# Neighbourhood attention with token tiles of sixteen rows by eight columns

## The chip, the core and the metric

The kernel runs on one core of a Trainium2 chip, with its five engines: TensorE (PE in the profile; PEld is its weight load), VectorE (DVE), ScalarE (ACT), GpSimd (POOL) and SyncE (SP), which mostly issues transfers. What is measured is the device time of one execution in microseconds. Lower is better.

## What is computed

Two layers of an encoder over 1024 tokens of width 1024. The tokens are a grid of 16 rows by 64 columns, counted row by row. Each layer takes one input projection apart into three mixers (latent attention MLA, six heads; neighbourhood attention NA, six heads; differential attention, four heads) and a gate for each, and ends with one output projection and a residual. What the change touches is NA:

```python
def neighborhood_attention(q, k, v, rpb, scale):
    kr = min(NA_KR_MAX, rows)          # 8 of 16 rows
    kc = NA_KC                         # 16 of 64 columns
    col_start = jnp.clip(col - kc // 2, 0, GRID_W - kc)
    col_idx = col_start[:, None] + jnp.arange(kc)[None, :]
    dc = col_idx - col[:, None] + (NA_KC - 1)
    def one(r):
        r0 = jnp.clip(r - kr // 2, 0, rows - kr)
        k_r = lax.dynamic_slice_in_dim(kg, r0, kr, axis=1)[:, :, col_idx]
        v_r = lax.dynamic_slice_in_dim(vg, r0, kr, axis=1)[:, :, col_idx]
        dr = r0 + jnp.arange(kr) - r + (NA_KR_MAX - 1)
        bias = rpb[:, dr[:, None, None], dc[None, :, :]]
        s = jnp.einsum('bchd,brcjhd->bhcrj', q_r, k_r) * scale
        s = s + bias.transpose(0, 2, 1, 3)[None]
        p = jax.nn.softmax(s.reshape(B, H, GRID_W, kr * kc), axis=-1)
        return jnp.einsum('bhcrj,brcjhd->bchd', p, v_r)
```

So a query at row r and column c sees 8 rows by 16 columns of keys, with a bias by relative row and column. MLA and the differential attention see all 1024 keys with rotary embeddings by token number.

## The kernel before

**Tiles and stages.** A tile is 128 consecutive tokens, two grid rows, and there are eight. A layer runs through: input norm and latent projection; differential and key-value projections; differential attention with the gate's projection beside it; NA projections; NA; MLA; output projection. In the first layer the start is apart: eight tiles of x are loaded (L376), squared and scaled (L352, L354), transposed by PE (`start_turn`, L355 to L360) and modulated (`start_mod`), while the modulation's weights stream in on SP's queue. The rope table is one transfer of 128x8x32 on SP (L405).

**NA.** `NA_CHUNKS` (L39) gives each of the eight query tiles its first key tile and their count, 4 or 5, 36 a head in all. An item (`na_item`, L1000) is one head and one query tile. `first`: scores into PSUM S in two halves, two matmuls each (L1012 with the high part of the keys, L1013 with the low part); VectorE adds the table and finds the extreme (L1018); ScalarE takes the exponential with its sum (L1021); VectorE the reciprocal (L1023); GpSimd scales (L1024). `second`: PE transposes the probabilities, 128 columns at a time (L638), into PSUM T, and ScalarE copies them out (L138), a second time where there are five. `third`: the value matmuls (L1042), one per key tile, whose result is 64 rows, so that they use 64 of PE's 128 columns: those of the head's parity. `finish`: after four items VectorE multiplies the gate by the result (L1048). PSUM O holds one head's half at a time.

`na_table` (L951) makes a head's bias and mask table: two transfers (L963) on SP from `rpb_rep` in memory, GpSimd adds the column mask (L964), copies ten of the fourteen rows (L965) and fills what the inner tiles must not see (L966 to L968). Even heads use the buffers t4 and t2, odd heads the two raw buffers; so a table's buffer comes free when head h-2 has its last scores. `rpb_rep` is written earlier, in the differential projections, by one transfer a head on ScalarE's queue (L480), which repeats the bias 64 times. `na_forms` (L971) transposes queries and keys of the next head through PSUM F (L982, L996), and ScalarE and VectorE write their high and low parts (L983, L984, L138, L998).

**What sets the order.** The items are registered with keys by `at`, first 3 places ahead of second, a table 6 places ahead of its head, forms 4 ahead; a scheduler then places each engine's instructions by its own estimate of times. MLA's setup (`mla_setup`, L1071: two subtractions on GpSimd at L1094, the query table's transfer and scaling at L1098 and L1099) and its first head's forms stand among the last NA heads.

## Time and profile before

| | us |
|---|---|
| median of 3 runs (lowest, highest) | 1851.77 (1850.18, 1853.68) |
| profiled execution, its own time | 1856.72 |
| its span in the trace | 1854.9 |

| engine | busy us | share of the span |
|---|---|---|
| PE | 1720.4 | 93% |
| DVE | 1338.3 | 72% |
| ACT | 947.9 | 51% |
| POOL | 811.2 | 44% |

Times in the rows are microseconds from the span's start. Busy time of an engine is the union of its instructions; a PE timeline's "us" is the whole passage of a group, and since matmuls overlap, what a group costs PE is read from one start to the next.

### The profile page before, as it was taken

How to read it: one execution, taken by the hardware profiler on the slowest of the kernel's cores; microseconds unless marked ns; L12 is line 12 of the kernel's file. 1: busy time of each engine (PE TensorE's matmuls, PEld its weight loads, DVE VectorE, ACT ScalarE, POOL GpSimd, SP SyncE). 2: the span in 40 equal slices, each digit the busy share in tenths (PEclk: the TensorE clock that was granted, in tenths of full speed). 3: DMA queues.
4: the chain of work that ended last, by engine and by line, in shares of the span. 5: the costliest groups of instructions: out<-in, count | busy, mean ns of one | idle time of the engine just before them, and what ended most of it. 6: DMA issues, size and time to landing. Idle time of an engine off the chain costs nothing. (4 is left out here: it accounts for less than half of the span.)

```text
span 1854.9 us, 28846 instructions
## 1 busy us (share of the span) xinstructions
PE 1720.4 (93%) x10724; PEld 1471.2 (79%) x10724; DVE 1338.3 (72%) x2634; ACT 947.9 (51%) x1954; POOL 811.2 (44%) x756
## 2 busy tenths in 40 slices
PE   4998889989899999989998988899999999999998
PEld 3978667778798888978878877777889888898877
DVE  6879877765975679995576487778565656999742
ACT  6522577771057667753342227777512765776500
POOL 4422435533345545473225043555415564556532
PEclk9999899999999999999999989999999999999999
DMA  9356000104323101131232520001221140003022
GB/s 285 100 131 168 13 24 23 35 1 123 104 55 54 59 1 24 35 89 33 80 127 59 109 82 23 24 12 35 66 86 29 21 102 1 12 24 81 23 91 91
DMA packets 141036, 117.60 MB, mean 63 GB/s; under 512 B 39834, under 2 KB 126048, under 8 KB 140384
## 3 DMA queue, kind: packets, MB, share of 16 engines
q1 hardware_dynamic: 116716, 103.61, 19.1%
q0 software_dynamic: 12480, 6.29, 2.0%
q10 hardware_dynamic: 11700, 5.85, 1.7%
q8 instruction: 85, 1.39, 0.3%
q14 instruction: 55, 0.45, 0.1%
HBM read 97.91 MB, written 23.68 MB: 66 GB/s over the span
## 5 line engine op out<-in xcount | busy, mean ns | idle before, releaser
L138 ACT ACTIVATE R<-T 128x512 fp32r<-128x512 f32 (+1 forms) x336 | 180.8, 550 | 125.5 <-PE T L638 61.8
L620 PE MATMUL F<-R,Pb 128*128 128x512 f32 x766 | 233.8, 420 | 11.7 <-ACT sg L138 11.7
L620 PEld LDWEIGHTS F<-R,Pb 128*128 128x128 f32 x766 | 141.5, 197 | 48.3 <-ACT sg L138 18.6
L1182 POOL TENSOR_SCALAR Pb<-Pb,sm 128x1024 f32<-128x1024 f32 x96 | 110.4, 1151 | 138.3 <-DVE sm L1178 69.3
L731 DVE TENSOR_REDUCE sm<-S 128x1 f32<-128x1024 f32 x128 | 153.2, 1218 | 16.0 <-PE S L726 14.5
L653 DVE TENSOR_TENSOR R<-T,R 128x512 fp32r<-128x512 f32 x192 | 129.1, 681 | 21.0 <-ACT R L138 20.1
L1180 ACT ACTIVATE Pb<-S,sm,rs_q 128x1024 f32<-128x1024 f32 x96 | 115.6, 1204 | 30.1 <-DVE sm L1178 26.4
L1200 PE MATMUL O<-R,nd 128*128 128x256 f32 x768 | 118.3, 292 | 6.3 <-DVE R L653 6.2
L1042 PE MATMUL O<-R,n1v 128*64 128x128 f32 x864 | 120.0, 280 | 1.2 <-ACT R L138 1.2
L1177 DVE TENSOR_REDUCE sm<-S 128x1 f32<-128x1024 f32 x96 | 116.5, 1213 | 5.4 <-PE S L1174 5.2
L650 PE MATMUL T<-ident,Pb 128*128 128x128 f32 x768 | 112.1, 275 | 6.8 <-DVE R L653 6.8
L1024 POOL TENSOR_SCALAR Pb<-Pb,sm 128x512 f32<-128x512 f32 (+1 forms) x96 | 74.5, 780 | 93.2 <-DVE sm L1023 87.7
L1200 PEld LDWEIGHTS O<-R,nd 128*128 128x128 f32 x768 | 102.9, 191 | 13.3 <-DVE R L653 9.1
L1042 PEld LDWEIGHTS O<-R,n1v 128*64 128x64 f32 x864 | 91.1, 136 | 21.7 <-issue 11.1
L1306 POOL TENSOR_TENSOR raw<-sg,raw 128x512 fp32r<-128x512 f32 x32 | 50.0, 1562 | 120.4 <-DVE raw L1305 120.3
L650 PEld LDWEIGHTS T<-ident,Pb 128*128 128x128 f32 x768 | 89.8, 142 | 16.1 <-DVE R L653 5.0
L801 POOL TENSOR_TENSOR Pb<-raw,Pb 128x512 fp32r<-128x512 f32 x32 | 43.8, 1372 | 125.2 <-DVE Pb L800 87.9
L733 ACT ACTIVATE nd<-S,sm 128x1024 f32<-128x1024 f32 x64 | 71.4, 1116 | 47.9 <-DVE sm L731 47.0
L457 ACT ACTIVATE t<-T 128x512 f32<-128x512 f32 x32 | 19.2, 599 | 141.9 <-DVE n1k L933 73.3
L737 POOL TENSOR_SCALAR nd<-nd,sm 128x1024 f32<-128x1024 f32 x48 | 58.7, 1223 | 65.0 <-DVE sm L735 64.8
L733 ACT ACTIVATE sg<-S,sm 128x1024 f32<-128x1024 f32 x64 | 71.3, 1115 | 27.7 <-DVE sm L731 14.1
L1172 PE MATMUL S<-R 128*128 128x512 f32 x192 | 84.8, 443 | 0.3
(439 smaller groups left out, 5247.4 us busy)
## 6 DMA issues: line engine op xcount, KB each, us to landing
raw<-in_w_in_dram SPq DMA_DIRECT2D x32, 512.0 KB
t<-in_ada_w_dram SPq DMA_DIRECT2D x40, 256.0 KB
n1k<-in_w_out_dram SPq DMA_DIRECT2D x16, 512.0 KB
v_d<-n1k SPq DMA_DIRECT2D x16, 384.0 KB
nl<-in_ada_w_dram SPq DMA_DIRECT2D x24, 256.0 KB
nd<-v_d POOLq DMA_DIRECT2D x12, 512.0 KB, 4.9
rpb_rep<-in_na_rpb_dram ACTq DMA_DIRECT2D x12, 476.2 KB
R<-in_ada_w_dram SPq DMA_DIRECT2D x8, 512.0 KB
```

Source lines behind the costliest of these rows:

```text
L138: A.activation(o, i, AF.Copy, scale=scale)
L620: ins = fn()
L650: PE.transpose(pt[:, i * 128:(i + 1) * 128], src_cols(i), ident)
L653: V.tensor_tensor(lo4, pv, f(hi4), ALU.subtract)
L731: V.tensor_reduce(stt[:, m:m + 1], ps, AX.X, ALU.max, negate=True)
L733: A.activation(p, ps.rearrange("p (k n) -> p k n", k=8), AF.Exp, bias=stt[:, m:m + 1], accum_out=stt[:, 2 + m:3 + m])
L1042: PE.matmul(O[m:m + 64, qs], nv[:, c0 + i, h * 64:(h + 1) * 64], PTf[qb][:, i, qs], start=(i == 0), stop=(i == n - 1), skip_group_check=True)
L1172: PE.matmul(o, qhi[:, ts_], khi[:, ks], start=True, stop=False)
L1177: V.tensor_reduce(stt[:, 0:1], ps, AX.X, ALU.max, negate=True)
L1180: A.activation(p, ps, AF.Exp, bias=stt[:, 3:4], scale=rs, accum_out=stt[:, 1:2])
L1182: mla["g"] = G.tensor_scalar(p, p, stt[:, 2:3], 0.0, ALU.mult, ALU.add)
L1200: PE.matmul(box["o"], mla[f"v{e}"][:, k], mla["PT"][b][:, hl, k], start=(k == 0 and hl == 0), stop=(k == 7 and hl == 1))
```

## The change

The order of tokens inside the kernel changes: a tile is now eight grid columns by all sixteen rows (`token_tiles`), in which the token number is column group, row, column. A query tile then needs its own and the two neighbouring tiles of keys: `NA_CHUNKS` becomes 2, 3, 3, 3, 3, 3, 3, 2, in all 22 a head. x is still loaded in its own order, and the copies after the first transposes write it in the new order; the residual's x and the output go through a view with eight rows of 4 KB per 64 tokens. The rope table is loaded by sixteen transfers on ScalarE's queue, and the query's rope table is rearranged by GpSimd in eight pieces.

An item's scores are two matmuls (L1047, L1048 of the new file) of 384 or 256 columns. The transposes of an item are one group (L677) with one copy. The value matmuls (L1075) are issued on odd items only, for two query tiles at once, each into its own half of PE's columns; PSUM O holds a whole head, and `finish` is two products at the end of the head. The table has 384 columns for inner tiles and 384 for the two outer ones, made from one transfer and four GpSimd operations with a row mask and a column mask (L1002, L1004), and uses one buffer of 768. `rpb_rep` is filled from a packed copy by two transfers a head.

```diff
-NA_CHUNKS = [(0, 4), (0, 4), (0, 5), (1, 5), (2, 5), (3, 5), (4, 4), (4, 4)]
+NA_CHUNKS = [(0, 2), (0, 3), (1, 3), (2, 3), (3, 3), (4, 3), (5, 3), (6, 2)]
...
+        return ap.rearrange("(r g c) d -> g r c d", g=8, c=8)
+    x_t = token_tiles(x)
+    x_n = x.rearrange("(t p) d -> t p d", p=128)
+    out_t = token_tiles(out)
...
-        copy_act(stage[k][:, th * 512:(th + 1) * 512], ps)
+        copy_act(stage[k].rearrange("p (g r c) -> p g r c", g=8, c=8)[:, :, th * 8:th * 8 + 8],
+                 ps.rearrange("p (r g c) -> p g r c", g=8, c=8))
...
-    nc.sync.dma_start(ropet, rope)
-    cmask = T(cp, "cmask", [128, 64])
-    nc.sync.dma_start(cmask, colmask)
+    for t in range(8):
+        src = rope[:, t].rearrange("(r g c) n -> r c g n", r=2, c=8)
+        for r in range(2):
+            nc.scalar.dma_start(ropet[t * 16 + r * 8:t * 16 + r * 8 + 8], src[r])
+    cmask = T(cp, "cmask", [128, 24])
+    rmask = T(cp, "rmask", [128, 16])
+    def na_masks():
+        rm = T(cp, "t2", [128, 640])[:, 0:32]
+        cm = lambda o, *ap: bass.AP(tensor=colmask.tensor, offset=colmask.offset + o, ap=[list(i) for i in ap])
+        nc.sync.dma_start(cmask, cm(8 * 64, (0, 16), (64, 8), (1, 24)))
+        for half in range(2):
+            nc.sync.dma_start(rm[half * 64:(half + 1) * 64], cm(half * (48 * 64 + 32), (128, 8), (0, 8), (1, 32)))
+        G.tensor_copy(rmask, rm.rearrange("p (j two) -> p j two", two=2)[:, :, 0])
+    def rpb_copies(i):
+        base, pk = rpb_rep[i], rpb_pk[i * 15:i * 15 + 1]
+        for c, n, run in ((0, 7, 513), (7, 1, 536)):
+            dst = bass.AP(tensor=base.tensor, offset=base.offset + 513 * c, ap=[[8 * 512 + 31, 16], [513, n], [1, run]])
+            src = bass.AP(tensor=pk.tensor, offset=pk.offset, ap=[[0, 16], [0, n], [1, run]])
+            nc.scalar.dma_start(dst, src)
...
-            for half in range(2):
-                src = bass.AP(tensor=base.tensor, offset=base.offset + 63 + (1 - half) * 64 * 127,
-                              ap=[[126, 64], [64 * 127, 14], [1, 64]])
-                nc.sync.dma_start(te[half * 64:(half + 1) * 64], src)
-            G.tensor_tensor(te, te, cmask.unsqueeze(1).to_broadcast([128, 14, 64]), ALU.add)
-            G.tensor_copy(tm, te[:, 2:12])
+            src = bass.AP(tensor=base.tensor, offset=base.offset + 7 * 31 + 7, ap=[[512, 128], [31, 16], [1, 24]])
+            nc.sync.dma_start(tr.rearrange("p (j y) -> p j y", y=24), src)
+            for d in range(3):
+                G.tensor_tensor(te[:, d], tr.rearrange("p (j y) -> p j y", y=24)[:, :, d * 8:d * 8 + 8],
+                                rmask.unsqueeze(2).to_broadcast([128, 16, 8]), ALU.add)
+            G.tensor_tensor(ti, te, cmask.rearrange("p (d x) -> p d x", x=8).unsqueeze(2).to_broadcast([128, 3, 16, 8]), ALU.add)
...
-                for a in range(2):
-                    ks = slice(c0 * 128 + a * w, c0 * 128 + (a + 1) * w)
-                    PE.matmul(ps[:, a, 0:w], q[:, p * 128:(p + 1) * 128], khi[:, ks], start=True, stop=False)
-                    PE.matmul(ps[:, a, 0:w], q[:, p * 128:(p + 1) * 128], klo[:, ks], start=False, stop=True)
+                ks = slice(c0 * 128, c0 * 128 + w)
+                PE.matmul(ps, q[:, p * 128:(p + 1) * 128], khi[:, ks], start=True, stop=False)
+                PE.matmul(ps, q[:, p * 128:(p + 1) * 128], klo[:, ks], start=False, stop=True)
...
+                O = obox["na", h][:, p // 2 * 128:(p // 2 + 1) * 128]
+                for i in range(3):
+                    for t in (p - 1, p):
+                        c, m = NA_CHUNKS[t]
+                        if i < m:
+                            PE.matmul(O[t % 2 * 64:t % 2 * 64 + 64], nv[:, c + i, h * 64:(h + 1) * 64],
+                                      PTf[qb][:, i, t % 4 * 128:(t % 4 + 1) * 128], start=(i == 0), stop=(i == m - 1),
+                                      skip_group_check=True)
...
-            tabq = T(cp, "t4", [128, 1024])
-            nc.sync.dma_start(tabq, ropeq)
-            G.tensor_scalar(tabq, tabq, vT[l][:, 41:42], 0.0, ALU.mult, ALU.add)
+            mla["x"] = T(bp, "n1k", [128, 3, 1024])
+            tabq, raw = T(cp, "t4", [128, 1024]), mla["x"][:, 2]
+            nc.sync.dma_start(raw, ropeq)
+            for g in range(8):
+                G.tensor_scalar(tabq[:, g * 128:(g + 1) * 128].rearrange("p (r c) -> p r c", c=8),
+                                raw.rearrange("p (r g c) -> p g r c", g=8, c=8)[:, g], vT[l][:, 41:42], 0.0, ALU.mult, ALU.add)
```

On PE, in the middle of layer 0's NA, before: O takes the value matmuls of L1042, T the transposes of L638, S the scores, F the next head's keys.

```order
L1012 MATMUL S_5033<-R_489_4537 128x256
L1013 MATMUL S_5033<-R_489_4537 128x256
L996 MATMUL F_5058<-ident_75,R_503_4675 128x128 x2
L638 MATMUL T_4994<-ident_75,Pb_4674 128x128 x4
L1042 MATMUL O_4950<-R_503_4675,n1v_3907 64x128 x8
L638 MATMUL T_5000<-ident_75,Pb_4674 128x128
L1012 MATMUL S_5087<-R_489_4537 128x256
L1012 MATMUL S_5111<-R_489_4537 128x256
L1042 MATMUL O_4950<-R_503_4675,n1v_3907 64x128 x4
L638 MATMUL T_5018<-ident_75,Pb_4674 128x128 x4
L996 MATMUL F_5065<-ident_75,R_503_4675 128x128 x4
```

The same place after, where L1075 are the value matmuls, L677 the transposes, L1047 and L1048 the scores and L1032 the next head's keys:

```order
L677 MATMUL T_4944<-ident_76,Pb_4704 128x128 x3
L1075 MATMUL O_4924<-R_505_4705,n1v_3937 64x128 x5
L1047 MATMUL S_4968<-R_491_4567 128x256
L1048 MATMUL S_4968<-R_491_4567 128x256
L677 MATMUL T_4957<-ident_76,Pb_4704 128x128 x3
L1075 MATMUL O_4924<-R_505_4705,n1v_3937 64x128
L677 MATMUL T_5005<-ident_76,Pb_4704 128x128 x3
L1032 MATMUL F_4991<-ident_76,R_505_4705 128x128 x4
L1075 MATMUL O_4924<-R_505_4705,n1v_3937 64x128 x5
L1075 MATMUL O_4924<-R_506_4706,n1v_3937 64x128
```

Groups of four or eight value matmuls of one query tile have become runs of five and one, of two tiles, and the transposes and scores of several items stand between them.

On GpSimd around a table, before (L964 adds the column mask, L965 copies, L966 to L968 fill, L1024 scales the probabilities):

```order
L1024 TENSOR_SCALAR Pb_4674<-Pb_4674,sm_5449 128x512
L964 TENSOR_TENSOR raw_5639<-raw_5639,cmask_543 128x896
L1024 TENSOR_SCALAR Pb_4674<-Pb_4674,sm_5474 128x512
L965 COPY raw_5640<-raw_5639 128x640
L1024 TENSOR_SCALAR Pb_4674<-Pb_4674,sm_5528 128x512
L966 MEMSET raw_5640 64x128
L967 MEMSET raw_5640 64x64
L968 MEMSET raw_5640 64x64
L1024 TENSOR_SCALAR Pb_4674<-Pb_4674,sm_5552 128x512
```

After, the last scalings of head 1 (L1056), the table of head 5 in the raw buffer (L1002, L1004) and the first scalings of head 2:

```order
L1056 TENSOR_SCALAR Pb_4704<-Pb_4704,sm_4933 128x384
L1056 TENSOR_SCALAR Pb_4704<-Pb_4704,sm_4952 128x384
L1056 TENSOR_SCALAR Pb_4704<-Pb_4704,sm_4971 128x256
L1002 TENSOR_TENSOR raw_5424<-raw_5424,rmask_560 128x128 x3
L1004 TENSOR_TENSOR raw_5424<-raw_5424,cmask_559 128x384
L1056 TENSOR_SCALAR Pb_4704<-Pb_4704,sm_5013 128x256
L1056 TENSOR_SCALAR Pb_4704<-Pb_4704,sm_5032 128x384
L1056 TENSOR_SCALAR Pb_4704<-Pb_4704,sm_5045 128x384
```

The table's operations, which stood between scalings, now stand together between the last scaling of one head and the first of the next.

On ScalarE at the program's start, before (L161 belongs to the modulation, L352 squares a tile of x, L294 and L295 are its norm):

```order
L161 ACTIVATE ssb_92<-csb_90 128x8
L352 ACTIVATE S_123,st_122<-n1q_97 128x1024
L294 ACTIVATE st_122<-st_122 128x1
L352 ACTIVATE S_134,st_133<-n1q_97 128x1024
L295 ACTIVATE st_122<-st_122 128x1
L294 ACTIVATE st_133<-st_133 128x1
L295 ACTIVATE st_133<-st_133 128x1
L352 ACTIVATE S_145,st_144<-n1k_98 128x1024
```

After, where L418 are the rope table's transfers, L359 the squares, L301 and L302 the norm:

```order
L418 DMA rope_542<-in_rope_t_dram 8x8x32 x2
L168 ACTIVATE ssb_93<-csb_91 128x8
L418 DMA rope_542<-in_rope_t_dram 8x8x32 x4
L359 ACTIVATE S_124,st_123<-n1q_98 128x1024
L418 DMA rope_542<-in_rope_t_dram 8x8x32 x2
L301 ACTIVATE st_123<-st_123 128x1
L359 ACTIVATE S_135,st_134<-n1q_98 128x1024
L418 DMA rope_542<-in_rope_t_dram 8x8x32
L302 ACTIVATE st_123<-st_123 128x1
L418 DMA rope_542<-in_rope_t_dram 8x8x32
L301 ACTIVATE st_134<-st_134 128x1
L418 DMA rope_542<-in_rope_t_dram 8x8x32
```

Sixteen transfers have come to stand between the squares and norms of the first tiles.

## Rows read from the trace of the kernel before

**Rows 1.** busy us (instructions) of PE, PEld, DVE, ACT, POOL by window; PEclk, DMA
```profile
25.00:50.00 25.00, 13.69 (x65) 12.00 (x63) 24.71 (x59) 14.48 (x29) 12.90 (x13) 1.00 1.00 271
250.00:400.00 150.00, 134.78 (x955) 107.47 (x952) 116.84 (x176) 112.70 (x203) 78.69 (x63) 0.99 0.08 22
531.00:664.00 133.00, 132.66 (x974) 110.02 (x973) 81.67 (x212) 88.65 (x200) 69.02 (x94) 1.00 0.19 43
664.00:845.00 181.00, 173.34 (x1140) 153.66 (x1139) 170.07 (x334) 124.77 (x241) 100.74 (x93) 0.99 0.15 38
1430.00:1564.00 134.00, 132.25 (x978) 110.31 (x976) 80.04 (x211) 89.37 (x201) 68.78 (x92) 1.00 0.18 43
```

**Rows 2.** three NA heads by line and shape: busy us, mean ns | idle before
```profile
L1042 PE MATMUL O<-R,n1v 128*64 128x128 f32 x216 | 30.2, 280 | 0.0
...
L138 ACT ACTIVATE R<-T 128x512 f32<-128x512 f32 x24 | 14.3, 595 | 9.0 <-PE T L638 8.8
...
L1021 ACT ACTIVATE Pb<-Pb,sm 128x640 f32<-128x640 f32 x12 | 9.9, 824 | 2.2 <-DVE sm L1018 2.1
...
L1021 ACT ACTIVATE Pb<-Pb,sm 128x512 f32<-128x512 f32 x12 | 8.6, 717 | 1.0 <-DVE sm L1018 1.0
...
L138 ACT ACTIVATE R<-T 128x128 f32<-128x128 f32 x12 | 3.3, 275 | 4.9 <-PE T L638 4.8
```

**Rows 3.** PE's timeline in NA: start us, us, engine, line, operation, out<-in, count
```profile
576.52 1.09 PE L1042 MATMUL O<-R,n1v 128*64 128x128 f32 x8
577.54 0.66 PE L638 MATMUL T<-ident,Pb 128*128 128x128 f32 x4
577.95 0.36 PE L1012 MATMUL S<-R 128*128 128x256 f32 x1
...
578.27 0.28 PE L1012 MATMUL S<-R 128*128 128x256 f32 x1
578.39 0.28 PE L1013 MATMUL S<-R 128*128 128x256 f32 x1
578.60 0.65 PE L1042 MATMUL O<-R,n1v 128*64 128x128 f32 x4
```

**Rows 4.** PE's timeline in the NA projections
```profile
515.01 0.33 PE L447 MATMUL T<-nd,R 128*128 128x384 f32 x1
515.18 0.33 PE L448 MATMUL T<-nd,R 128*128 128x384 f32 x1
```

**Rows 5.** PE's timeline in the differential attention, value matmuls of two items
```profile
407.48 0.27 PE L764 MATMUL O<-nl,nd 128*64 128x128 f32 x1
407.49 0.27 PE L764 MATMUL O<-t,nd 128*64 128x128 f32 x1
407.59 0.27 PE L764 MATMUL O<-nl,nd 128*64 128x128 f32 x1
```

**Rows 6.** the chain that ended last, layer 1's differential attention: start us, us, what
```profile
1144.47 1.90 PE O L764 x32
```

**Rows 7.** POOL's timeline in layer 1's NA, a table between scalings
```profile
1444.19 2.09 POOL L964 TENSOR_TENSOR t<-t,cmask 128x896 f32<-128x896 f32 x1 [1.23 <-DMA t<-rpb_rep]
1446.35 1.06 POOL L965 COPY t<-t 128x640 f32<-128x640 f32 x1
```

**Rows 8.** SP's timeline, the same table's two transfers as issued
```profile
1439.78 1.28 SPq L963 DMA_DIRECT2D t<-rpb_rep  x2
```

**Rows 9.** line L1094: count, ns min/median/max, first and last start
```profile
L1094 POOL TENSOR_TENSOR n1q<-nl,n1q x2: 2358/2555/2752, 617.6 to 1515.1; 128x1024 fp32r<-128x1024 f32 x2
```

**Rows 10.** PE's timeline at the NA projections' first matmuls
```profile
505.72 0.59 PE L276 MATMUL O<-one,acc 128*128 128x1 f32 x2 [5.06 <-DVE mod L277]
...
506.95 0.52 PE L446 MATMUL T<-nd,R 128*128 128x384 f32 x1
507.27 0.52 PE L447 MATMUL T<-nd,R 128*128 128x384 f32 x1
```

**Rows 11.** line L480, the bias copies issued by ScalarE
```profile
L480 ACTq DMA_DIRECT2D rpb_rep<-in_na_rpb_dram x12: 841/847/1465, 113.4 to 1058.3; - x12
```

More of the change, by code (lines that the diff above doesn't have):

```diff
@@ L925, in hybrid_encoder_kernel @@
         tap(f"sg_{l}", sg)
+        if l == 0:
+            na_masks()
         Wnd = T(bp, "nd", [128, 6, 1024], F32R)
@@ L1031, in second @@
                 qs = slice(tq * 128, (tq + 1) * 128)
[L1032 to L1033 removed]
+                transpose_plain(lambda i: pb[:, i * 128:(i + 1) * 128], PTf[qb][:, 0:n, qs], n, True)
             def third():
[L1036 to L1043 removed]
+                if p == 1:
+                    obox["na", h] = psO()
+                O = obox["na", h][:, p // 2 * 128:(p // 2 + 1) * 128]
[6 more added lines that the diff above has]
+                                      skip_group_check=True)
             def finish():
                 m = 64 * e
[L1047 to L1050 removed]
+                g = sg[m:m + 64, 3 + h // 2].rearrange("p (t two n) -> p two t n", two=2, n=128)
+                for half in range(2):
+                    O = obox["na", h][half * 64:half * 64 + 64].rearrange("p (t n) -> p t n", n=128)
+                    V.tensor_tensor(g[:, half], g[:, half], O, ALU.mult)
+            return first, second, ([third] if p % 2 else []) + ([finish] if p == 7 else [])
         def nv_side(tt):
```

65 lines of the change are left out of this document (24 added, 41 removed).

## The prediction

> **What bounds the kernel now.** I read the busy shares by stage first, because the edit rebuilds one stage, the neighbourhood attention (NA), and touches the rest only at its edges. NA runs from its first score matmul to its last value matmul; the windows of [rows 1] hold it in whole microseconds (531 to 664, 1430 to 1564), and the matmuls fill 132.7 and 133.8 of them, a mean of 133.3 us a layer. In both windows TensorE (PE) is busy 132 of 133 to 134 us, while VectorE has some 60%, ScalarE 66% and GpSimd 51% [rows 1]. Over three heads in the middle of the stage the largest group, the value matmuls, never has PE idle ahead of it [rows 2]. So here the end is set by PE alone, and any column taken off PE is time, until another engine is as full.
>
> The PE timeline gives prices by start-to-start, which is what counts on a pipelined engine [rows 3]: the values of four chunks 1.02 us (.255 a chunk: each is two instructions, and writes only 64 of 128 columns), four transposes .41 (.10 each), the four score matmuls of a 256-wide item .65. Before has 36 chunks a head: 36 x .255 = 9.2 values, 36 x .10 = 3.7 transposes, 8 x .65 = 5.2 scores, and 16 transposes of L982/L996 at about .105 = 1.7, together 19.8 us. Six heads are 119; the other 14 us of the window are joins between groups (about 1 us a head) and eight small pieces of MLA's preparation (about 8 us).
>
> **The change, part by part.**
>
> *Tile shape.* A 16 by 8 tile sees 22 key chunks a head instead of 36. Transposes fall to 22 x .10 = 2.2. An item's scores become two matmuls of 384 (or 256) instead of four; a 384-wide one of the same kind is started every .17 us in another stage [rows 4], so 2 x .17 + .06 for the join is .41, and 6 x .41 + 2 x .29 = 3.0 a head.
>
> *Column halves.* Two query tiles of neighbouring key ranges go to the two halves of PE. Before does that already, in the differential attention: the two halves start 10 ns apart and the next pair .11 us later [rows 5], and 32 instructions (two items of eight chunks) take 1.90 us [rows 6], .2375 for a pair of chunks, which is less than a single chunk costs now. A head has 10 pairs and 2 single chunks: 10 x .2375 + 2 x .255 = 2.9 us in place of 9.2. In the new order the value groups are cut into runs of five and one, with other work between. A 256-wide item takes .65 though its matmuls are .12 apart [rows 3], so going from one kind of work to the next costs .18; nine such joins a head are 1.6 us.
>
> PE then has 2.9 + 2.2 + 3.0 + 1.7 + 1.6 = 11.4 us a head; I use 11.45.
>
> *The other engines.* ScalarE: the exponential takes .72 at 512 and .82 at 640 columns [rows 2], so by that slope .61 at 384 and .50 at 256, and .10 more for reading the accumulator: 6 x .71 + 2 x .60 = 5.5. Copies out of PSUM take .60 for 512 and .28 for 128 columns [rows 2], so .49 and .38: 3.7 for eight. The forms stay at four of .60 to .68, 2.5. Neighbouring instructions overlap by a tenth, as they do in this stage now, which leaves 10.7 a head. VectorE: of its 12.2 us a head now (82 over six heads, with MLA's pieces, [rows 1]) only L1018 shrinks, by its columns: 9.5 to 11. GpSimd: of its 11.5 us a head now (69 over six heads, [rows 1]) a table takes about 3.2 and MLA's setup some, and the scaling, the rest, falls with the columns (22 chunks for 36) to 4.5 or so. So PE stays the longest, but with ScalarE at 93% of it, no longer two thirds. A stage as full as that has joints: the differential attention runs VectorE at 78%, ScalarE at 75% and gets PE to 90% [rows 1]; MLA gets 96% with VectorE at 94% [rows 1]. I charge .9 us a head (8%): 12.35.
>
> *Tables.* A table is one transfer instead of two, and on GpSimd 768 columns in four instructions instead of 1536 in two with three small fills: half of 3.15 us (L964 and L965, [rows 7]), with the fixed costs about 2. What does not shrink is the wait: the buffer comes free with the last scores of two heads before, the transfer is issued at 1439.78 [rows 8], and GpSimd starts on it at 1444.19 after 1.23 us of standing still [rows 7]: 4.4 us. Before hides this behind 20.8 us a head of PE work. In the new order the tables of heads 2, 5 and 4 stand on GpSimd right behind the last scaling of heads 0, 1 and 2, so the scalings of the next head queue behind a transfer not yet landed: GpSimd is blocked some 5 us, PE has about two items' work in hand (2 x 1.45 = 2.9 us), so 2 to 3 us of PE are lost, three times a layer: 6 us. MLA's setup puts L1130's two subtractions (L1094 now, of which the first kind takes 2.55 us, [rows 9]; 5 for both) and eight pieces of the query table between scalings of one head: 3 us more.
>
> By the pieces the transfer could be slower too. The Trainium skill (DMA: Bandwidth & Descriptors, the table at its head) gives 512 bytes as the least for the full rate; the table's pieces go from 256 to 96 bytes and from 1792 to 2048. If time goes by pieces, an estimate from that count is 14% more, 4.4 to 5.0 us, which would add about 4 us to the sum. No row before shows a piece of 96 bytes.
>
> *Clock.* Behind 5.06 us of idle PE the granted clock is at its lower level (1.2 GHz): the same 384-wide matmul is started every .32 us, against .17 [rows 4, 10]. One such stretch a layer, where PE idles at a table or at the first items, is 2 us.
>
> *NA after:* 6 x 12.35 + 8 (MLA pieces, unchanged) + 6 + 3 + 2 = 93 us for 133.3, a gain of 40.2 a layer, 80.4 in all.
>
> *Start.* The rope table's sixteen small transfers stand at the head of ScalarE's queue, between the squares of the first norms; in the new order the fourth tile's norm falls behind the first weight casts. A transfer issued by ScalarE costs .85 us at L480 [rows 11], which has far more pieces than one of these; sixteen are at most 14 us of ScalarE, and none of it need be on the path, for ScalarE has free time there: from 25 to 50 us it is busy 14.5 of 25, while VectorE is at 24.7 and the DMA share at 1.00 [rows 1]. So 0 to +10; I take +4, nearer to the lower end, since VectorE and the transfers set that stage. The permuted writes of the transposed x keep their size: 0 (up to +2).
>
> *Edges.* The mask loads and GpSimd's copy of 128x16 stand ahead of the NA projections, and sit in slack of about 5 us: +1 (0 to +3). The query table in pieces is counted above. The bias copies move 262 KB a head instead of 476: 0 (down to -2). Strided residual and output transfers keep pieces of 4 KB: 0.
>
> **Sum.** 1856.7 (the profiled execution's own time, its span being 1854.9) - 80.4 + 4 + 1 = 1781.3. The profiled run lies 4.95 above the median of 1851.77; taking that off, **1776 us**.
>
> **The rivals.**
>
> *ScalarE and VectorE become the bound.* If ScalarE can be had only at the 75% of the differential attention [rows 1], a head is 10.7 / .75 = 14.3 us; 85.6 + 8 + 9 (tables and setup, partly inside) = 102.6, a gain of 30.7 a layer: 1795. For it: the chain scores, minimum, exponential, reciprocal, scaling, transposes, copy, values crosses four engines, and items are shorter with fixed costs unchanged. Against: MLA's 94 to 96%. This is what the Trainium skill says of such tiling (TensorEngine Tiling (Array Packing), PSUM Bottleneck: it "speeds up TensorE but not PSUM evacuation"); the share of 75% is the row's. .25.
>
> *PE fed without a break.* Tables and joints hidden, as now: 6 x 11.45 + 8 = 76.7, a gain of 56.6 a layer, with +4 at the start: 1743. Against it is how little cover three short items give. .12.
>
> *The halves do not run together here,* for they read other weights and write one bank with other tiles between: 10 pairs x .27 = 2.7 us a head, +33: 1809. Rows 5 speak against. .06.
>
> *The start costs more,* each of the sixteen issues a full .85 on the path: +15 instead of +4, 1787. .04.
>
> *Slower: PE at the lower clock through NA.* PE no longer always busy could fall to 1.2 GHz, as behind the idle stretch in [rows 10], and stay there with gaps at every head: 2 x 11.45 = 22.9 a head, 6 x 22.9 + 16 = 153.4 for 133.3, +40 +5: 1896. It decides against the change when about 55% of the heads run so (the gain of 75 over 12 x 11.45). Against: the differential attention with PE at 90% keeps .99 [rows 1]. .06, of which .04 as far as slower and .02 halfway, near no change.
>
> **How the numbers follow.** Forecast .47, the rivals .25, .12, .06, .04, .06. The range reaches over the first, third and fourth rival: 1742 to 1810. A change under 0.2% (3.7 us) cannot be told from none here. Slower .04, same .02, faster .94.
>
> **What would show it.** Right: NA windows near 93 us, PE 85 to 90% busy in them, value pairs 10 ns apart at .24 us; GpSimd standing still 3 to 5 us for three tables a layer. If PE is under 80% and ScalarE or VectorE over 85% without waits on tables, the first rival; over 97%, the second. Value groups at .5 us for a pair, the third. A first score matmul of NA later than about 536 us puts more on the start. Granted clock well under .95 in the NA windows, the last. Wrong altogether if the windows shrink and MLA or the output projection grow by as much.

## The result and the profile after

The changed kernel takes 1796.66 us (median of 4 runs, 1794.52 to 1801.36) where the kernel before takes 1852.51 on the same chip: a ratio of 0.9705, 95% interval 0.9687 to 0.9722, a gain of 56 us. The forecast was 1776 us with a range of 1742 to 1810, a gain of 76. So the direction and the range hold, and 20 us of the expected gain did not come. The profiled execution took 1795.2 us, its span is 1793.1; that of before stood 4 us above its median, so the two profiles differ by 62 us and not 56.

Cut at starts of PE's lines, the two profiled executions stand like this (us; the neighbourhood attention, NA, is counted from the first score matmul with the low part of the keys, L1013 or L1048, to the last value matmul, and "hand-over and MLA" from there to the first matmul of the output projection):

| stretch | before | after | difference | forecast |
|---|---|---|---|---|
| start to NA, layer 0 | 531.3 | 529.2 | -2.1 | +5 |
| NA, layer 0 | 132.2 | 92.0 | -40.2 | -40.2 |
| hand-over and MLA, layer 0 | 185.5 | 197.7 | +12.2 | 0 |
| output projection, layer 0 | 103.6 | 103.6 | 0 | 0 |
| from there to NA, layer 1 | 477.9 | 473.5 | -4.4 | 0 |
| NA, layer 1 | 132.9 | 93.4 | -39.5 | -40.2 |
| hand-over and MLA, layer 1 | 187.7 | 198.3 | +10.6 | 0 |
| output projection and end | 104.0 | 105.5 | +1.5 | 0 |

NA gave what was reckoned. Right behind it 23 us were given back. (The differences of 2 and 4 us ahead of NA are no larger than what the profiles of other kernels show: the second stretch lies between 472.3 and 478.3 in all the kernels below, whatever their edit.)

Of the changed kernel, the busy times by window: its NA windows, the 19 us behind each, and the rest of layer 0's MLA (columns as in [rows 1]):

```profile
529.00:621.00 92.00, 82.31 (x597) 60.19 (x599) 60.98 (x202) 64.06 (x170) 50.84 (x81) 0.96 0.22 46
621.00:640.00 19.00, 15.47 (x70) 11.70 (x69) 11.95 (x26) 8.20 (x16) 8.79 (x14) 0.82 0.00 0
640.00:815.00 175.00, 167.47 (x1101) 149.52 (x1100) 161.91 (x318) 119.47 (x229) 96.70 (x90) 0.98 0.16 39
1395.00:1489.00 94.00, 84.46 (x601) 62.64 (x600) 60.48 (x201) 64.98 (x170) 49.66 (x81) 0.95 0.22 46
1489.00:1508.00 19.00, 15.09 (x76) 11.80 (x76) 12.82 (x27) 9.13 (x18) 9.63 (x14) 0.91 0.00 1
```

And the kernel before in the same 19 us behind its NA:

```profile
664.00:683.00 19.00, 18.94 (x118) 16.35 (x117) 17.91 (x40) 13.12 (x28) 10.50 (x11) 1.00 0.00 1
1564.00:1583.00 19.00, 18.96 (x118) 16.35 (x116) 17.91 (x40) 13.11 (x26) 10.66 (x11) 1.00 0.01 1
```

Read the second row against the sixth. Before, PE is busy 18.94 of 19 us at full clock and VectorE 17.91: MLA is in full swing when NA ends. After, PE is busy 15.47 with a granted clock of 0.82, and VectorE 11.95. These two set MLA's pace (167 and 162 of 175 us in the third row), and VectorE lost 6 us here.

Inside NA PE is no longer always busy: 82 of 92 us, against 132 of 133 [rows 1]. ScalarE is at 70%, VectorE at 66%.

The prices of the prediction, read again. Five chunks (ten instructions) of two tiles in column halves, and the scores beside them, in PE's timeline of the changed kernel:

```profile
604.82 0.44 PE L1047 MATMUL S<-R 128*128 128x384 f32 x1
605.10 0.34 PE L1048 MATMUL S<-R 128*128 128x384 f32 x1
605.38 0.87 PE L1075 MATMUL O<-R,n1v 128*64 128x128 f32 x10
606.18 0.44 PE L1047 MATMUL S<-R 128*128 128x384 f32 x1
```

The ten take .80 us to the next start, .16 a chunk; before a chunk took .255 [rows 3]. The two score matmuls of 384 columns ahead of them start .28 apart, and the second starts .28 before the values: .56 for the item, where .41 was reckoned. With like work beside them it is different, at another place of the same timeline:

```profile
549.28 0.76 PE L677 MATMUL T<-ident,Pb 128*128 128x128 f32 x5
549.80 0.42 PE L1047 MATMUL S<-R 128*128 128x384 f32 x1
550.06 0.33 PE L1048 MATMUL S<-R 128*128 128x384 f32 x1
550.23 0.34 PE L1047 MATMUL S<-R 128*128 128x384 f32 x1
550.40 0.34 PE L1048 MATMUL S<-R 128*128 128x384 f32 x1
550.59 0.60 PE L1018 MATMUL F<-ident,n1q 128*128 128x128 f32 x4
```

Behind transposes the first pair is .26 apart, the next starts follow by .17, as in [rows 4]. Shorter groups mean more such joins between one kind of work and the next.

### The profile page after: what moved, and what is told of

Read it like the earlier page. It is cut to its first block, busy times and chain, and to the rows that moved or that the text cites. A ratio compares the mean times of both kernels' runs of the same rounds, so it can differ in the third digit from the quotient of the medians.

```text
span 1793.1 us, 27407 instructions
## 1 busy us (share of the span) xinstructions
PE 1628.7 (91%) x10028; PEld 1378.8 (77%) x10028; DVE 1303.8 (73%) x2634; ACT 904.3 (50%) x1906; POOL 783.0 (44%) x759
## 5 line engine op out<-in xcount | busy, mean ns | idle before, releaser
L140 ACT ACTIVATE R<-T 128x512 fp32r<-128x512 f32 (+2 forms) x288 | 153.6, 551 | 94.5 <-PE T L689 68.7
L1210 PE MATMUL S<-R 128*128 128x512 f32 x192 | 86.8, 454 | 0.6
L1056 POOL TENSOR_SCALAR Pb<-Pb,sm 128x384 f32<-128x384 f32 (+1 forms) x96 | 53.6, 568 | 61.3 <-DVE sm L1055 50.2
L1211 PE MATMUL S<-R 128*128 128x512 f32 x192 | 78.9, 411 | 0.0
L1212 PE MATMUL S<-R 128*128 128x512 f32 x192 | 78.6, 411 | 0.0
```

What stands on the lines that cost most here:

```text
L140: A.activation(o, i, AF.Copy, scale=scale)
L1210: PE.matmul(o, qhi[:, ts_], khi[:, ks], start=True, stop=False)
L1211: PE.matmul(o, qhi[:, ts_], klo[:, ks], start=False, stop=False)
```

## Experiments

Each run is compared with the kernel before on the same chip; ratios are to it. What decides most of them are two numbers a layer from the trace: the length of the NA window, and of what follows up to the output projection.

### Where the 23 us went: MLA's preparation

The theory formed from the table: MLA's first heads are prepared during NA by a chain that begins when NA's last head has read its queries (their buffer, n1q, takes MLA's latent). In the changed kernel the transposes that read them end at 596.87, and the chain starts .19 us later on VectorE (the timelines' columns are start us, us, engine, line, operation, out<-in, count, idle before):

```profile
597.06 1.34 DVE L1129 CAST n1q<-nl 128x1024 fp32r<-128x1024 f32 x2
```

On GpSimd, the two subtractions, the first pieces of the query table, and the first keys:

```profile
597.88 2.73 POOL L1130 TENSOR_TENSOR n1q<-nl,n1q 128x1024 fp32r<-128x1024 f32 x1 [0.63 <-DVE n1q L1129]
600.57 2.36 POOL L1130 TENSOR_TENSOR nd<-nl,n1q 128x1024 fp32r<-128x1024 f32 x1
602.91 0.73 POOL L1137 TENSOR_SCALAR t<-n1k,vT 128x128 f32<-128x128 f32 x2
...
609.59 2.08 POOL L1185 TENSOR_TENSOR n1k<-nl,rs_k 128x512 f32<-128x512 f32 x2 [0.16 <-DMA nl<-nk_d]
```

On SP, the reload of MLA's keys as it is issued:

```profile
602.96 0.33 SPq L1132 DMA_DIRECT2D nl<-nk_d  x1
```

And on PE, the first query projection and the first scores of MLA:

```profile
612.77 0.49 PE L1158 MATMUL F<-n1q,nd 128*128 128x512 f32 x1
...
618.79 0.50 PE L1210 MATMUL S<-R 128*128 128x512 f32 x1
```

From the cast of the latent (L1129, 597.06) over the two subtractions (to 602.9), the reload of the keys (issued at 602.96, used at 609.59) and the query projection (612.77) to MLA's first score matmul (618.79) are 21.7 us. In the kernel before, VectorE's cast is here:

```profile
616.78 1.29 DVE L1093 CAST n1q<-nl 128x1024 fp32r<-128x1024 f32 x2
```

and PE's first score matmul of MLA here, 28.0 us later:

```profile
644.81 0.48 PE L1172 MATMUL S<-R 128*128 128x512 f32 x1
```

The chain became no longer. But NA's last value matmul comes 46.7 us after the cast before (663.5), and 24.1 us after it now (621.2). I call this the cover: the part of NA behind which the preparation can run.

**e5: the kernel before with the chain begun late.**

```diff
+                rec = V.reciprocal(stt[:, 2:3], stt[:, 1:2])
+                if (h, p) == (5, 3):
+                    na_hold[0] = rec
...
-                (V.tensor_copy if OPT["mla"]["lat"] == "V" else copy_act)(hi, latq[:, kc])
+                with tc.issue_after(na_hold[0].ins):
+                    V.tensor_copy(hi, latq[:, kc])
...
```

> The kernel before, with the first step of MLA's preparation (L1093) queued on VectorE behind the reciprocal of the last head's fourth item, so that the chain begins about 25 us before the end of the neighbourhood attention and not 46.7, as in the changed kernel (24.1). Nothing else is changed. Cover theory: the time from the last value matmul to the output projection grows as it did in the changed kernel, 8 to 12 us a layer, 16 to 24 in all: 1868 to 1878 where the kernel before takes 1852 to 1855. Rival (the loss comes from something else in the change): within 4 us of the kernel before.

Measured: 1872.92 us (1867.81 to 1873.89) beside 1852.40, ratio 1.0098 (1.0075 to 1.0122). The cast came at 639.84, where the last queries had been read at 619.99, and the cover was 20 us. NA became 7 us shorter a layer (MLA's pieces left it), what follows 18 and 15 us longer: 203.2 and 202.9; together 10 and 8 us a layer, as the cover theory had it. Not all that grows behind NA is lost: from one start of PE to the next, MLA's pieces take 9.0 us of NA's window in the kernel before, .5 in e5 and 5.0 in the changed kernel, and what leaves the window is done behind it. So some 9 and 7 us a layer are lost in e5, and some 8 and 7 of the 12.2 and 10.6 in the changed kernel; the other 4 are work that moved. The window behind NA in layer 0 of e5 looks like that of the changed kernel:

```profile
660.00:679.00 19.00, 14.62 (x61) 11.10 (x60) 10.70 (x25) 5.45 (x13) 7.98 (x13) 0.83 0.00 1
```

Without a line of the change in it, the old kernel shows the same loss, PE at 14.6 of 19 us and the clock at 0.83. The rival, that something in the change itself has to do it, falls.

**e4: the chain begun early.** The queries of an even and an odd head share the 128 columns that are transposed; one transposition now makes both heads' query forms, into spare form buffers, so n1q is free a head and a half earlier.

```diff
+        def na_q(h):
+            return forms[:, (0, 3, 6, 7, 0, 3)[h]]
...
-            for th in range(2 if 0 in part else 0):
+            for th in range(2 if 0 in part and e == 0 else 0):
...
-                A.activation(q[m:m + 64, ns], ps[m:m + 64], AF.Copy, scale=gq)
-                V.scalar_tensor_tensor(q[o:o + 64, ns], ps[m:m + 64], gq, f(q[m:m + 64, ns]), ALU.mult, ALU.subtract)
+                for m, o in ((0, 64), (64, 0)):
+                    q, gq = na_q(h + m // 64), vT[l][m:m + 64, 40:41]
+                    A.activation(q[m:m + 64, ns], ps[m:m + 64], AF.Copy, scale=gq)
+                    V.scalar_tensor_tensor(q[o:o + 64, ns], ps[m:m + 64], gq, f(q[m:m + 64, ns]), ALU.mult, ALU.subtract)
...
```

> The changed kernel with the query forms of two heads made from one transposition of their 128 common columns (two spare form buffers take them), so the last queries are read a head and a half earlier; MLA's preparation may begin that much earlier, and PE has 24 transposes a layer less (2.6 us). Cover theory: the first MLA scores come well before the last values of the stage, and of the 11 to 12 us a layer 8 to 11 come back; with the transposes 9 to 13 us a layer, 18 to 26 in all, 1771 to 1779. Rival (the loss has nothing to do with when the chain begins): only the transposes, 2 to 5 us in all, 1792 to 1795.

Measured: 1782.28 us (1777.58 to 1782.71), ratio 0.9596 (0.9576 to 0.9617), the changed kernel 0.9705. The cover is 43.7 us, and what follows NA takes 186.8 and 187.2 us, as in the kernel before (185.5, 187.7). NA itself holds more of MLA's pieces again (11.1 us) and takes 95.8 and 92.9. The windows of e4, layer 0's NA and the 19 us behind each layer's:

```profile
531.00:627.00 96.00, 87.91 (x608) 63.98 (x606) 64.58 (x212) 66.15 (x176) 57.47 (x93) 0.95 0.23 45
627.00:646.00 19.00, 18.30 (x113) 15.20 (x110) 18.56 (x39) 12.41 (x24) 7.88 (x9) 1.00 0.00 1
...
1488.00:1507.00 19.00, 18.29 (x114) 15.15 (x115) 18.56 (x38) 12.40 (x24) 8.16 (x9) 1.00 0.01 2
```

PE 18.30 of 19 at full clock, VectorE 18.56: the hand-over is whole again. By its time it came out 3 us above the expected range, but the kernel before was slower on that chip too; by the ratios e4 is 20 us faster than the changed kernel, within the 18 to 26 expected. The sum of NA and what follows fell by 7 and 12 us a layer, where 9 to 13 were expected. Not all of that need be the cover's: three heads' query transposes are gone too, 24 at about .105 (the prediction's price), some 2.5 us of PE a layer.

**e3: the two subtractions L1130 on VectorE,** which was meant to shorten the chain.

```diff
-                G.tensor_tensor(lo, latq[:, kc], f(hi), ALU.subtract)
+                V.tensor_tensor(lo, latq[:, kc], f(hi), ALU.subtract)
```

> The changed kernel with the two subtractions of MLA's latent low parts (L1130) on VectorE, not on GpSimd. From the last value matmul of the neighbourhood attention to the first matmul of the output projection the changed kernel takes 197.7 and 198.3 us, before 185.6 and 187.6: 12 and 11 us of the gain are given back there. Theory (cover): MLA's preparation is a chain of fixed length that begins when the last head's queries have been read, 46.7 us before the end of the stage in the kernel before and 24.1 now, and what it lacks in cover is the loss. The subtractions take 5.1 us of the chain on GpSimd, and some 2.2 on VectorE: 2 to 4 us a layer less, 4 to 8 in all, 1789 to 1793. Rival (the loss is the half clock at the hand-over or the query table in eight pieces): no change within 2 us.

Measured: 1796.15 us beside 1855.13, ratio 0.9682 (0.9655 to 0.9708), which overlaps the changed kernel's interval. What follows NA is 2.2 and 0.9 us shorter (195.5, 197.4), and NA 1.3 and 0.7 longer. The edit did not shorten the chain: from the cast to MLA's first scores it takes 22.5 us in both layers, in the changed kernel 21.7 and 22.5. On VectorE the subtractions stand between NA's own work, and the keys' reload is issued 5.1 us behind the cast, where it was 5.9. So e3 does not test the theory.

**The cover in all kernels.** The cast's start, the last value matmul and the output projection's first matmul were read from every profiled execution, layer 0 and layer 1:

| kernel | cover | from the last value matmul to the output projection |
|---|---|---|
| before | 46.7, 50.0 | 185.5, 187.7 |
| e5, before with a late chain | 20.0, 20.8 | 203.2, 202.9 |
| changed | 24.1, 24.9 | 197.7, 198.3 |
| e1 (below) | 27.0, 27.0 | 197.1, 197.6 |
| e2 (below) | 24.3, 24.4 | 196.5, 197.4 |
| e3, subtractions on VectorE | 25.4, 25.4 | 195.5, 197.4 |
| e10 (below) | 37.4, 37.3 | 194.4, 195.6 |
| e9 (below) | 41.4, 41.7 | 186.2, 185.8 |
| e11 (below) | 41.4, 41.4 | 185.5, 187.6 |
| e7 (below) | 41.0, 43.7 | 188.4, 187.2 |
| e4, forms by pair | 43.7, 43.7 | 186.8, 187.2 |
| e6 (below) | 48.9, 45.0 | 184.7, 190.9 |
| e8 (below) | 48.5, 49.0 | 185.7, 188.5 |
| e12 (below) | 48.6, 49.3 | 185.7, 187.0 |

With 41 us or more MLA takes 185 to 189 us (once 191), with 37 it takes 194 to 196, with 20 to 27 it takes 195 to 203.

### What the column halves are worth

**e1: tile after tile in the changed kernel.**

```diff
-                for i in range(3):
-                    for t in (p - 1, p):
+                for t in (p - 1, p):
+                    for i in range(3):
```

> The changed kernel with the value matmuls in another order: all chunks of one query tile, then all of the other, so that no two neighbouring ones use different halves of the columns. Theory that the halves run together and that PE sets the pace of the neighbourhood attention: ten pairs a head cost .51 us in place of .24, 2.7 us a head, 32 us over twelve heads; some of it falls into PE's idle 10 us a layer, so 20 to 32 us slower than the changed kernel, 1817 to 1829. Rival, that the gain is the tile's shape and other engines set the pace: under 8 us slower.

Measured: 1808.14 us beside 1855.13, ratio 0.9731 (0.9704 to 0.9757), where the changed kernel has 0.9705: some 5 us more in all, with intervals that overlap. That is what the rival expected, not the theory's 20 to 32. In the profiles the NA windows are 97.1 and 98.6 us, 5 more each. Added up from one start to the next, the 264 value matmuls of layer 0's window take 33.3 us (.25 a chunk, as before) against 25.2, and 55.9 in the kernel before: the halves are worth 8 us, half of the 16 that sixty pairs at .27 would give. Three of the 8 did not lengthen the window. PE's idle time in it fell from 9.7 to 8.75 us and MLA's pieces from 5.0 to 4.0; where the rest went was not traced:

```profile
532.00:629.00 97.00, 88.25 (x593) 67.88 (x592) 61.79 (x202) 64.11 (x169) 50.02 (x81) 0.96 0.22 44
```

**e11: the same in the kernel with forms by pair.**

> The kernel with query forms by pair, and the value matmuls tile after tile as in e1. In e1 the windows grew by 5 us a layer, of 16 reckoned. If that was all that running the halves together saves: again 4 to 6 us a layer, 1790 to 1795. If a part of it was hidden behind PE's waits, which the pair has fewer of: 8 us a layer or more, 1798 or more.

Measured: 1782.35 us, ratio 0.9610 (0.9596 to 0.9624), beside 0.9596 for e4: no difference clear of noise. The windows are 94.8 and 94.8 us, against 95.8 and 92.9. So most of the value matmuls' gain is the tile's shape, 22 chunks for 36; the halves bring 5 us a layer to the window of the one kernel and nothing that can be seen in the other. The expectation of at least 4 us a layer fell: 5 us of value matmuls less (31.9 to 27.0 by starts in layer 0) shorten nothing. The Trainium skill (TensorEngine Tiling (Array Packing), PSUM Bottleneck) says that tiling speeds up TensorE but not the emptying of PSUM. This trace agrees as far as that PE's time alone does not count; that the emptying of PSUM is what does, no run shows.

### What sets the pace inside NA now

The largest waits of layer 0's window in the changed kernel, of all engines (engine, line, what it waited for, us in total, times, longest):

```profile
POOL Pb L1056 <- DVE sm L1055: 26.9, 18, 5.5
ACT R L140 <- PE T L677: 10.1, 18, 1.0
DVE Pb L1052 <- PE S L1048: 8.9, 10, 2.6
POOL raw L1002 <- DMA raw<-rpb_rep: 6.4, 2, 5.2
PEld S L1047 <- DVE sm L1052: 6.3, 10, 1.6
PEld O L1075 <- ACT R L140: 5.1, 14, 0.8
```

The first three belong to engines that are busy 55 to 70% of the window. Of the 6.4 us at tables 5.2 lie ahead of GpSimd's first scaling. PE's own largest waits, those of its weight load (PEld), are the last two: scores that wait for VectorE to free a score buffer, and value matmuls that wait for ScalarE's copies.

**e6: four score tiles instead of two,** on top of the forms by pair: two items share a score buffer of two banks.

```diff
-                ps = psS()[:, 0:w]
+                if p % 2 == 0:
+                    sbox[0] = psS()
+                ps = sbox[0][:, p % 2 * 512:p % 2 * 512 + w]
...
```

> The kernel with query forms by pair, and two items of the neighbourhood attention sharing one score buffer of two banks, so that four score tiles can be open and not two. In the trace of the changed kernel PE's waits for VectorE to free a score buffer add up to 10 us in layer 0's window, the largest of its waits. Theory that these waits set the pace of what is left: 5 to 10 us a layer, 10 to 20 faster than with the pair alone (1782), 1762 to 1772. Rival, that the next wait (value matmuls for ScalarE's copies, forms for their one PSUM bank) comes in their place: under 5 us in all.

Measured: 1778.32 us (1773.47 to 1786.62), ratio 0.9598 (0.9563 to 0.9634) beside 0.9596: no difference. NA and what follows add up to 280.2 and 280.3 us, against 282.6 and 280.1. In layer 0's window PE and its weight load wait 3.7 us for score buffers in e6 and 6.8 in e4; PE stands for another thing instead, which is not among e4's waits:

```profile
PE O L1082 <- DVE sg L1091: 4.2, 3, 3.0
```

The rival holds: the wait changed places (here the value matmuls wait for VectorE's final products to free PSUM's one output bank).

**e9: tables kept.** Heads 2 to 5 use the tables of heads 0 and 1, so their own are left out.

```diff
-                na_tabs[h] = na_table(h)
+                na_tabs[h] = na_table(h) if h < 2 else na_tabs[h - 2]
```

> The kernel with query forms by pair (1782), in which heads 2 to 5 take the tables of heads 0 and 1: four table transfers and their GpSimd work a layer are left out, so the bias of those heads is wrong. The prediction charged 6 us a layer for GpSimd standing still at tables. If that is so: 5 to 8 us a layer less in the windows of the neighbourhood attention (95.8 and 92.9 with the pair alone), 1766 to 1772. Rival (GpSimd has room, the waits shown there are 0.3 to 1.2 us): under 2 us a layer, 1778 to 1782.

Measured: 1774.58 us (1773.74 to 1775.83), ratio 0.9566 (0.9550 to 0.9581) beside 0.9596. The windows are 91.1 and 90.5 us, 4.7 and 2.4 less than with the pair alone, and with what follows 5.3 and 3.8 less. So by the profiles the four tables of a layer cost 4 to 5 us, where 6 were charged; by the ratios the whole kernel gains 5.6 us, with intervals that just overlap. The first window of e9:

```profile
535.00:626.00 91.00, 83.63 (x604) 61.75 (x604) 63.40 (x211) 65.95 (x176) 48.09 (x77) 0.98 0.17 39
```

GpSimd has 48 us of work in the window instead of 57 (e4's first row). e9 takes the tables' work, transfers and waits away together, so it does not say which of them costs. That it is the work between scalings, more than the standing still that the prediction named, is argued from the waits: the three tables that it named wait .29, 1.22 and 0 us in layer 0 of the changed kernel and .58, .46 and 0 in layer 1. The first of them, that of head 2 behind head 0, is here in POOL's timeline,

```profile
544.19 1.61 POOL L1002 TENSOR_TENSOR t<-t,rmask 128x128 f32<-128x128 f32 x3 [0.29 <-DMA t<-rpb_rep]
545.88 1.01 POOL L1004 TENSOR_TENSOR t<-t,cmask 128x384 f32<-128x384 f32 x1
546.86 1.05 POOL L1056 TENSOR_SCALAR Pb<-Pb,sm 128x256 f32<-128x256 f32 x2
```

and its transfer, issued at 541.07, is there 3.1 us later, where two transfers of longer pieces took 4.4 [rows 7, 8]; it moves 192 KB, those two 448 KB. The prediction's estimate of 5.0, from the count of pieces, is not borne out. It stood beside the Trainium skill's least size for the full rate (DMA: Bandwidth & Descriptors, Specifications), of which this says nothing, since the pieces of before (256 bytes) and of after (96) both lie under it.

**e10: no scaling,** except on each head's last item.

```diff
-                ins = G.tensor_scalar(pb[:, 0:w], pb[:, 0:w], stt[:, 2:3], 0.0, ALU.mult, ALU.add)
+                if p == 7:
+                    ins = G.tensor_scalar(pb[:, 0:w], pb[:, 0:w], stt[:, 2:3], 0.0, ALU.mult, ALU.add)
...
```

> The kernel with query forms by pair, in which GpSimd scales only each head's last item, so the division by the softmax's sum is left out elsewhere: the chain from scores to transposes is one engine shorter (about .6 us of work and a hand-over an item). PE stands still or behind some 10 us a layer in the windows of the neighbourhood attention. Theory that the length of this chain sets the pace where PE waits: 4 to 9 us a layer less, 1764 to 1774. Rival (PE's own work, with joins between short groups, is the pace): under 2 us a layer, 1778 to 1782.

Measured: 1782.17 us (1774.97 to 1785.16), ratio 0.9602 (0.9577 to 0.9627): the time of the pair alone, as the rival had it, but not for the rival's reason. The windows did shrink, to 85.1 and 87.7 us, 10.7 and 5.2 less (2.8 of it MLA's pieces, 8.3 us where e4 has 11.1); what follows grew to 194.4 and 195.6, 7.6 and 8.4 more. Layer 0's windows of e10:

```profile
533.00:618.00 85.00, 78.51 (x585) 57.91 (x584) 58.59 (x203) 62.98 (x170) 30.56 (x48) 1.00 0.26 51
618.00:637.00 19.00, 15.65 (x94) 13.39 (x95) 15.70 (x34) 10.07 (x20) 5.83 (x7) 0.91 0.00 0
```

The chain through GpSimd is a part of NA's pace, and once NA is shorter MLA's preparation has less cover again (37 us): the second row shows PE at 15.65 of 19 and a clock of 0.91. The gain of the window is paid back at the hand-over a second time; that the cover is the reason here too fits the table above and was not tested by itself.

### The start, and a better version

**e2: the rope transfers on SP's queue.**

```diff
-            nc.scalar.dma_start(ropet[t * 16 + r * 8:t * 16 + r * 8 + 8], src[r])
+            nc.sync.dma_start(ropet[t * 16 + r * 8:t * 16 + r * 8 + 8], src[r])
```

> The changed kernel with the sixteen transfers of the rope table on SP's queue, behind the weights, where the one transfer stood before. Theory that they cost the start what its latent projection lost (it ends at 92.0 us instead of 88.9): 3 us faster, 1794, or what is left of it. Rival, that the differential attention, which begins no later than before (203.6 for 204.1), takes the 3 us up again: no change within 2 us.

Measured: 1804.88 us beside 1855.13, ratio 0.9723 (0.9705 to 0.9740): no gain, rather 3 us lost, though the interval overlaps that of the changed kernel. The latent projection ends at 97.9 us instead of 92.0.

**e7: the rope transfers later on ScalarE's queue,** behind the last modulation, with the forms by pair.

```diff
-            nc.scalar.dma_start(ropet[t * 16 + r * 8:t * 16 + r * 8 + 8], src[r])
+            with tc.issue_after(last_mod[0].ins):
+                nc.scalar.dma_start(ropet[t * 16 + r * 8:t * 16 + r * 8 + 8], src[r])
...
```

> The kernel with query forms by pair, and the sixteen rope transfers queued on ScalarE behind the last modulation of x, out of the first 40 us. Theory that they cost the start 3 us (the latent projection ended at 91.9 us, before at 88.9) and the end sees it: 2 to 4 us faster than the pair alone, 1778 to 1780. Rival, that the differential attention's start takes it up: within 2 us of 1782.

Measured: 1787.14 us beside 1852.40, ratio 0.9638 (0.9614 to 0.9661), slower than the pair alone (0.9596, up to 0.9617). The projection ends at 96.8 us. Both kernels have the start's early transposes back, and both put PE behind VectorE's sums of the modulation's weights, in order, with the projection's matmuls queued behind, as PE's timeline of e2 shows:

```profile
49.82 1.01 PE L267 MATMUL O<-one,n1q 128*128 128x1 f32 x4 [2.59 <-DVE n1q L265]
...
67.96 1.01 PE L267 MATMUL O<-one,n1q 128*128 128x1 f32 x4 [8.25 <-DVE n1q L265]
```

The granted clock differs too: from 50 to 75 us PE is busy 16.75 us in e2 at 0.67 and 15.86 in e7 at 0.73, in the changed kernel 21.01 at 0.93.

In ScalarE's timeline of the changed kernel the norms (L301) stand behind rope transfers in its queue, and the idle time ahead of three of them ends with a rope transfer, but early:

```profile
7.65 0.20 ACT L301 ACTIVATE st<-st 128x1 f32<-128x1 f32 x1 [0.87 <-DMA rope<-in_rope_t_dram]
...
10.60 0.20 ACT L301 ACTIVATE st<-st 128x1 f32<-128x1 f32 x1 [1.18 <-DMA rope<-in_rope_t_dram]
...
16.00 0.20 ACT L301 ACTIVATE st<-st 128x1 f32<-128x1 f32 x1 [2.25 <-DMA rope<-in_rope_t_dram]
```

So the price of the transfers by themselves was not found: moving them changes the scheduler's order of the whole start, and the projection then ends 5 to 6 us later. How much of that is the order and how much the clock was not separated.

**e8 and e12: parts together.** e8 is forms by pair, four score tiles, later rope transfers and the low parts on VectorE; e12 the same without the rope edit.

> Query forms by pair, four score tiles, rope transfers later and the low parts on VectorE together. If the parts add: 1782 less 10 to 20 for the scores, 2 to 4 for the rope table, and for the low parts 0 to 3 (the chain now has cover): 1756 to 1770. If the waits only change places: 1774 to 1782.

Measured: 1786.16 us, ratio 0.9635 (0.9616 to 0.9655): above both expected ranges, and as slow as e7 (0.9638), whose rope edit it holds.

> Query forms by pair, four score tiles, and MLA's two low-part subtractions on VectorE. GpSimd loses 5.1 us a layer just where MLA's preparation stands between the last scalings; leaving out the tables' GpSimd work there (e9) gave 5 and 4 us a layer over the stage and the hand-over. Theory that GpSimd's queue at the hand-over still sets the sum of the two: 3 to 5 us a layer less than with the four score tiles (1778), 1768 to 1773. Rival (VectorE, which takes the work, is as late): within 2 us of 1778.

Measured: 1783.41 us (1776.00 to 1784.67), ratio 0.9609 (0.9587 to 0.9631): nothing beyond the forms by pair. The best version that computes everything is that edit, 0.9596, or e6, 0.9598; they cannot be told apart, and both are 1% under the changed kernel. e9 (0.9566) is faster and e10 as fast, but both leave a part of the computation out.

## Why the prediction was right, and where it missed

**The bound and NA's new length.** That PE alone set the pace of the old NA was right, and so was the window of 93 us (measured 92.0 and 93.4, or 92.5 and 94.3 from the first score matmul to the end of the last value matmul, as the prediction counts). PE is busy 89% of it, as forecast. That PE with a little loss at joints would also set the new NA's pace holds only in part: in e11 5 us more of it cost nothing, and in e10 a shorter chain through GpSimd shortened the window. The terms inside do not agree as well as their sum. Priced from one start on PE to the next, with the waits in them, a head's values take 25.2 / 6 = 4.2 us (2.9 and a part of 1.6 for joins reckoned), its transposes 20.9 / 6 = 3.5 (2.2), its scores 27.8 / 6 = 4.6 (3.0), the forms of the five heads in the window 13.3 / 5 = 2.7 (1.7), and MLA's pieces 5.0 in all (8). More went into joins and small waits than the .9 and 1.6 a head, less into stalls at tables, and 3 to 4 us of MLA's pieces left the window. So it came out even by luck in part: the sum was better than its parts.

**The step that failed** is "8 (MLA pieces, unchanged)" in the sum, and with it that everything behind NA stays as it is. The pieces were 5.0 us and not 8, and behind NA it took 12.2 and 10.6 us more, 23 in all, a little more than the 20 that are missing; some 8 and 7 of them are time lost and the rest the pieces that moved. MLA's preparation hung on the last head's queries, and NA shorter by 40 us a layer took half of its cover; e5 shows it in the kernel before, e4 takes it away. The prediction's last sign, windows that shrink while MLA grows by as much, named the place, as something that would make it wrong altogether: it came to 23 of 80 us. The trace of before had the chain in view: its cast at 616.78, 28 us ahead of MLA's first scores, in a stage whose end the change moves towards it.

**Column halves.** They run together (in the run at 605.38 the two halves of a pair start 7 ns apart), but 2.7 us a head was too much by far: e1 gives 8 us of PE and 5 of the window a layer, not 16, and e11 no time at all. In short runs a chunk takes .16 and not half of .2375. The rival "the halves do not run together" was therefore priced much too high (+33).

**Tables.** 6 us a layer charged, 4 to 5 measured in the windows (e9); GpSimd stood still 1.5 and 1.0 us a layer at the three tables, not some 5 at each, so the reason was for the most part wrong. The 3 us for MLA's setup were not measured by themselves.

**Clock.** One stretch of 2 us a layer was charged. The windows show 0.96 and 0.95, and the 19 us behind them 0.82 and 0.91. A mean of 0.96 is 8% of the time at the lower of the two levels, where a 384-wide matmul is started every .32 us and not .17 [rows 4, 10]. As an estimate from these rows that is at most 92 x .04 = 3.7 us inside NA, and 19 x .18 = 3.4 at the hand-over, less where PE would have stood still anyway. From 25 to 50 us of the start, for which nothing was charged, the granted clock is 0.66, before 1.00 [rows 1].

**Start and edges.** The projection ended 3.0 us later (4 reckoned; over the profiles it ends at 88.9 and 90.5 with the old start and at 89.7 to 92.5 with the new one), but NA does not begin later: at 529 to 535 us in the kernels that keep the changed start, at 531.3 before and 534.9 in e5. What the start loses is not seen in the end.

**The rivals.** ScalarE and VectorE as the bound gave 1795, nearly the measured time, but by another mechanism, so the agreement is a coincidence: the windows are 92 and not 102.6 us, with ScalarE at 70%. PE without a break did not come: 82 of 92. The start at +15 did not come. PE at the lower clock throughout did not come.

## What to carry to other kernels

When a stage is made shorter, look at what used it as cover: find the chain that prepares the next stage, see which event starts it and how long it is, and how much of its cover the shorter stage leaves. Here 41 us or more left what follows about as long as it was, and 24 lost 7 to 8 us a layer. Of 80 us 23 came back behind NA that way, some 15 of them lost and the rest work that moved, and an edit that starts the chain earlier brought 20 back, some 5 of them by the transposes that it saves. A new layout of the work should be credited by experiment to its parts: of the 40 us a layer in this one the column halves brought 5 at most; the rest is the other parts together, above all the 22 chunks a head in place of 36.

## What the runs showed of the hardware

Two score matmuls of 384 columns start .17 us apart beside their like and .26 to .28 apart behind transposes or values. The Trainium skill (TensorEngine Tiling (Array Packing), Key Properties) says that a change of the tiling mode drains TensorE. That would fit the values, which use 64 columns, but the trace shows .26 behind transposes too, which use the whole array as the scores do, so the mode is not all of it. PE left with gaps at a hand-over, busy 14.6 to 16.0 of 19 us, was granted 0.73 to 0.91 over these 19 us in each kernel with a cover of 37 us or less; busy 17.8 or more, it was granted 1.00 in each with 41 or more. With sixteen small transfers taken from the head of ScalarE's queue the latent projection ended 5 to 6 us later and not earlier, in the order that the scheduler then chose (e2, e7).
